# Norm's factor squared and applied after the down projections, seven products in another order, one plain block of features for two

## The chip, the cores and the metric

One core of a Trainium2 chip runs the whole program. The metric is the device time in microseconds (us) of one execution; the time before is the median of three runs.

## The reference, cut to what matters

A trunk of two layers runs on 768 tokens (512 and 256). Each layer is an attention block and then this block, in float32:

```python
    h = rmsnorm(x, ln_mlp[layer])          # x * rsqrt(mean(x*x)) * gain, over 1024 features
    x = x + jnp.square(jax.nn.relu(h @ w_up[layer])) @ w_down[layer]
return rmsnorm(x, ln_f)
```

`w_up` is 1024 x 4096, `w_down` 4096 x 1024. A token's factor r of the norm is positive, so square(relu(r*v)) = r*r*square(relu(v)).

## The kernel before, in words

Features lie on the 128 partitions, tokens in the free dimension: `x[k]` is 128 features by 768 tokens, k = 0 to 7. The tokens are two halves A and B of 384. Every float32 product is made of three matmuls on halves (hi x hi, hi x lo, lo x hi); `wsplit` (L76) makes weight halves `whi` on ACT (L80) and `wlo` on DVE (L81), `halve` (L114) makes those of activations (ACT L116, DVE L117).

**Up stage** (L820 to L955). 16 blocks `mp` of 256 features. A block of two by two (features, tokens) over two halves of the 1024 inputs is 8 plain products of 12 matmuls, or 7 by Strassen and Winograd's scheme (`product`, L855, matmuls at L861). The first two blocks are plain (L902), because the scheme's operands `comb[4..7]` are made meanwhile by `second` (L804, subtractions at L797, halves at L116 and L117); the other 14 are made from 7 products (L928 on). POOL makes the weight sums of a block (L846), DVE adds the products up in the tile `z` (adds at L869, L952; one ACT copy at L934), and `finish` (L875) follows: DVE's max with 0 and times R, the norm's factor of each token (L880), ACT's square (L882), a store to T in HBM from ACT's queue (L883), DVE's three sums `ta`, `tb` (L889 to L891) and two stores from POOL's queue (L893). R needs the sum of squares of all x: `nm.add` (squares on ACT at L147, adds on DVE at L152) stands ahead of the blocks, `rstd` (L161, L166, L167) and `bcast` (L185) between the halves of the plain blocks, R's copy at L177.

**Down stage** (L959 to L1052). Seven products in ORDER 1, 2, 7, 4, 5, 6, 3, each of NG = 4 steps of 48 matmuls (L1027) into four PSUM banks r. `operand` (L920) loads T and halves it (tile `th`, three buffers), `halves` (L993) halves weights (four `whi`, two steps' worth), `sums` (L987) makes POOL add into the kept weights in place (L991), so that a sum waits until DVE has read the weights for the product before. After a product's last step the four banks are folded into x (L1031 to L1048): 48 DVE instructions of 128x384 and 4 ACT copies in a layer.

**Ends.** Layer 0 goes on with splits of x (L119, L120) and the next norm's squares; `sq2` takes their tiles in turn from two tags, one of them "R". Layer 1 ends with `final`, half by half: the first half beside the steps of the last product, the second after it.

The instructions of each engine run in the order that the framework has chosen at compile time, by its own estimate of when each is ready and by the program's order; the trace shows it (DVE's rows of several blocks interleave).

Of the kernel before, what the change touches and what calls it, by code (L numbers as in the profile page):

```python
# [37 lines left out]
def kernel(ctx: ExitStack, tc: tile.TileContext, a: dict, y: bass.AP):  # L38
# [735 lines left out]
    def mlp(layer, src, o, x, es):  # L774
# [6 lines left out]
        sq = lambda: xo_tile("sq")  # L781
        two = [0]

        def sq2():
            two[0] ^= 1
            return xo_tile("sq") if two[0] else cpool.tile([P, NT], F32, tag="R", name="sq", bufs=1)

        nm = Norm(sq2)
# [82 lines left out]
        R, wait, done = [], [], list(range(FF // 256))  # L871

        T = [dram.tile([P, 7, ND, HT], F32, name=f"T{layer}_{i}") for i in range(NG)]

        def finish(z):  # L875
# [23 lines left out]
        ws = [weights(True) for _ in range(2)]  # L899
        for k in MO:  # L900
            nm.add(x[k])
        for w in ws:  # L902
# [10 lines left out]
            if len(wait) == 1:  # L913
                w2 = weights()
                second()
        R.append(nm.spread(rt))
# [11 lines left out]
        for mp in range(2, FF // 256):  # L928
            w = weights() if mp > 2 else w2
# [6 lines left out]
            if mp == FF // 256 - 1:  # L936
# [3 lines left out]
                ths = [operand(1, 0)]  # L940
            add(z12, one(6), z11)
            add(z11, p2, z11)
            if mp == 2:
# [5 lines left out]
            if mp == 2:  # L949
# [3 lines left out]
            add(z12, p5, z12)  # L953
            finish(z)
        g2s.close()  # L955
# [16 lines left out]
        def fetch(n, i):  # L972

            for rp in PR:
                off = (((layer * NG + i) * 4 + (11, 22, 21, 12).index(BLOCK[n])) * 2 + rp) * P * 1024
                if n in (1, 4) and (n, i) != (1, 0):
                    t = ch.tile([P, 1024], F32, tag="ch", name="ch", bufs=8)
                else:
                    third[0] += n != 1
                    if n == 1 or third[0] % 3 == 0:  # L980
# [18 lines left out]
        def fold(out, x_, op=ALU.add):  # L999
            add(out, out, x_, op)  # L1000

# [6 lines left out]
        for s, (n, i) in enumerate(steps):  # L1008
# [20 lines left out]
            if i == NG - 1:  # L1029
                for r, ps in enumerate(banks):  # L1030
                    x12, x11, x22, x21 = (xb(r, m_, sl) for m_ in PR for sl in (A, B))  # L1031
# [4 lines left out]
                    if n == 4:  # L1036
                        fold(x21, ps)
                    if n in (7, 5):
                        fold(x22, ps, ALU.subtract)
                    if n == 7:  # L1040
                        fold(x21, ps, ALU.subtract)
                    if n in (5, 3):
                        fold(x12, ps)
                    if n == 6:
                        fold(u[:, r], ps)
                        fold(x21, u[:, r], ALU.subtract)
                        fold(x22, u[:, r], ALU.subtract)
                        fold(x12, u[:, r])  # L1048
            if layer == 1 and n == 3 and i < NG - 1:
                last[0](i)  # L1050
            elif layer == 1 and n == 6 and i == NG - 1:
                last = [final(x, lambda: acs.tile([P, HT], F32, tag="sq", name="sq", bufs=4), s_) for s_ in (HT, 0)]  # L1052
# [8 lines left out]
        es = open_hl()  # L1061
        nxt, nn = [None] * KD, Norm(sq2)
# [8 lines left out]
    def final(x, sq, s):  # L1071
# [186 lines left out]
```

## Time and profile before

| | us |
|---|---|
| median of 3 runs (1742.3 to 1744.41) | 1743.85 |
| the profiled execution | 1743.15 |
| its span in the trace | 1741.4 |
| up stage, layer 0 (first L861 to first L1027) | 361.7 to 610.0 |
| down stage, layer 0 | 610.0 to 847.4 |
| up stage, layer 1 | 1238.5 to about 1488 |
| down stage, layer 1, and end | to 1741.4 |

PE is the matmul engine, PEld its weight loads, which run beside matmuls; DVE, ACT, POOL and SP are the other engines; a q behind a name is its queue of DMA issues. In a row of the timeline the bracket gives the idle time of the engine just before the row, and what ended it. "x4" is four instructions in one row.

### The profile page before, as it was taken

The numbers are of one execution on the slowest core, as the hardware profiler recorded it, in microseconds if no ns is written. First come the engines' busy times: TensorE is split into PE (matmuls) and PEld (weight loads), VectorE is DVE, ScalarE is ACT, GpSimd is POOL, SyncE is SP. The second block draws the span as 40 slices with busy tenths as digits, with TensorE's granted clock in tenths as the row PEclk, the third lists the DMA queues.
The fourth block names the chain that finished last, engine by engine and source line by source line (L and its number), as shares of the span: only waits on it lengthen the run. The fifth ranks groups of instructions, "written<-read, shape, count | busy, mean of one in ns | idle before, by whom it ended". The sixth has DMA issues, their size and how long they took to land.

```text
span 1741.4 us, 28288 instructions
## 1 busy us (share of the span) xinstructions
PE 1710.9 (98%) x10988; PEld 1622.0 (93%) x10988; DVE 1396.1 (80%) x2202; ACT 823.5 (47%) x1513; POOL 571.3 (33%) x435
## 2 busy tenths in 40 slices
PE   8999999999999999999999999999999999999997
PEld 8888888899999999999999999988999999999997
DVE  8888647499888888899566776775898898787994
ACT  7765434354333354444435555554543333544442
POOL 2200000034566414574021222210235655054751
PEclk9999999999999999999999999999999999999998
DMA  4111222414444687663310111112134445977621
GB/s 170 37 46 49 69 78 91 136 38 156 158 158 157 199 343 300 244 209 133 115 49 32 50 39 33 55 59 97 49 117 160 159 168 177 345 294 266 207 91 73
DMA packets 74597, 235.42 MB, mean 135 GB/s; under 512 B 7904, under 2 KB 25056, under 8 KB 74464
## 3 DMA queue, kind: packets, MB, share of 16 engines
q1 hardware_dynamic: 52480, 186.93, 31.4%
q0 software_dynamic: 7168, 25.17, 3.9%
q10 hardware_dynamic: 14816, 21.52, 3.4%
q8 instruction: 86, 1.41, 0.3%
q14 instruction: 47, 0.39, 0.1%
HBM read 182.47 MB, written 50.33 MB: 134 GB/s over the span
## 4 chain that ended last, share of the span: by engine, by line
PE 69%; DVE 19%; issue 6%; ACT 4%; POOL 1%; DMA 1%; POOLq 0%; DVEq 0%; ACTq 0%; SPq 0%
PE dn L1027 26%; PE dqk L196 8%; PE opa L208 5%; DVE z L880 4%; PE dvp L196 4%; DVE z L869 3%; DVE wlo L81 3%; PE npa L208 3%; PE opb L208 3%; DVE t L869 3%; DVE t L797 2%; ACT z L882 2%; PE ds L274 2%; PE dpv L721 2%; PE qp L196 2%
## 5 line engine op out<-in xcount | busy, mean ns | idle before, releaser
L861 PE MATMUL up<-c,whi 128*128 128x384 f32 x1824 | 467.3, 337 | 1.3 <-ACT z L911 1.3
L1027 PE MATMUL dn<-th,whi 128*128 128x384 f32 x1792 | 460.8, 338 | 0.0
L861 PEld LDWEIGHTS up<-c,whi 128*128 128x128 f32 x1824 | 330.3, 188 | 1.6 <-ACT z L911 1.5
L1027 PEld LDWEIGHTS dn<-th,whi 128*128 128x128 f32 x1792 | 325.7, 188 | 0.7 <-DVE th L117 0.5
L861 PE MATMUL up<-c,wlo 128*128 128x384 f32 x912 | 309.8, 340 | 4.9 <-DVE wlo L81 4.7
L1027 PE MATMUL dn<-th,wlo 128*128 128x384 f32 x896 | 302.9, 338 | 0.5 <-DVE wlo L81 0.5
L846 POOL TENSOR_TENSOR s<-wraw 128x512 f32<-128x512 f32 x56 | 104.1, 1877 | 420.3 <-DMA wraw<-in_w_up_dram 369.6
L991 POOL TENSOR_TENSOR ch<-ch,wd 128x1024 f32<-128x1024 f32 x60 | 189.1, 3161 | 117.0 <-DVE wlo L81 94.5
L81 DVE TENSOR_TENSOR wlo<-ch,whi 128x1024 fp32r<-128x1024 f32 x88 | 167.2, 1915 | 27.7 <-ACT whi L80 27.5
L861 PEld LDWEIGHTS up<-c,wlo 128*128 128x128 f32 x912 | 171.3, 188 | 12.4 <-DVE wlo L81 12.1
L80 ACT ACTIVATE whi<-ch 128x1024 fp32r<-128x1024 f32 x88 | 93.2, 1064 | 176.2 <-PE dn L1027 138.9
L1027 PEld LDWEIGHTS dn<-th,wlo 128*128 128x128 f32 x896 | 168.3, 188 | 1.1 <-DVE wlo L81 1.1
L117 DVE TENSOR_TENSOR th<-tr,th 128x1536 fp32r<-128x1536 f32 x56 | 142.3, 2544 | 12.0 <-ACT th L116 11.5
L81 DVE TENSOR_TENSOR wlo<-wraw,whi 128x1024 fp32r<-128x1024 f32 (+3 forms) x132 | 139.2, 1055 | 14.3 <-ACT whi L80 14.1
L80 ACT ACTIVATE whi<-wraw 128x1024 fp32r<-128x1024 f32 (+3 forms) x128 | 116.8, 914 | 55.3 <-PE opb L208 24.6
L882 ACT ACTIVATE z<-z 128x1536 f32<-128x1536 f32 x32 | 47.7, 1490 | 165.8 <-DVE z L880 165.8
L196 PE MATMUL dqk<-whi,xh 128*128 128x256 f32 x384 | 114.7, 299 | 0.0
L196 PE MATMUL dqk<-whi,xl 128*128 128x256 f32 x384 | 107.5, 280 | 0.0
L196 PE MATMUL dqk<-wlo,xh 128*128 128x256 f32 x384 | 107.2, 279 | 0.0
L706 ACT ACTIVATE de<-ds,m 128x512 f32<-128x512 f32 (+1 forms) x96 | 58.4, 613 | 81.7 <-DVE m L704 81.7
L116 ACT ACTIVATE th<-tr 128x1536 fp32r<-128x1536 f32 x56 | 82.7, 1477 | 23.2 <-DMA tr<-T 14.1
L869 DVE TENSOR_TENSOR z<-up,z 128x384 f32<-128x384 f32 x168 | 89.7, 548 | 0.1
(220 smaller groups left out, 3736.4 us busy)
## 6 DMA issues: line engine op xcount, KB each, us to landing
wd<-in_w_down_dram SPq DMA_DIRECT2D x84, 512.0 KB, 5.0
tr<-T SPq DMA_DIRECT2D x56, 768.0 KB, 5.6
wraw<-in_w_up_dram SPq DMA_DIRECT2D x64, 512.0 KB, 3.6
T<-t POOLq DMA_DIRECT2D x64, 384.0 KB, 3.0
T<-z ACTq DMA_DIRECT2D x32, 576.0 KB, 3.0
ch<-in_w_down_dram SPq DMA_DIRECT2D x28, 512.0 KB, 7.4
wraw<-in_w_in_o_dram SPq DMA_DIRECT2D x24, 512.0 KB, 3.6
wraw<-in_w_in_e_dram SPq DMA_DIRECT2D x16, 512.0 KB, 3.6
```

What stands on the lines that cost most here:

```text
L80: nc.scalar.activation(hi, raw, AF.Copy)
L81: nc.vector.tensor_tensor(out=lo, in0=raw, in1=hi.bitcast(F32), op=ALU.subtract)
L116: nc.scalar.activation(hi, src, AF.Copy)
L117: nc.vector.tensor_tensor(out=lo, in0=src, in1=hi.bitcast(F32), op=ALU.subtract)
L196: nc.tensor.matmul(ps[:, :256], st[:, tk], col(k, part, 0, 256), start=(k == 0 and i == 0), stop=(k == KD - 1 and i == 2))
L208: nc.tensor.matmul(ps[:, : e - s], w, mv[:, s:e], start=(k == 0 and i == 0), stop=(k == nk - 1 and i == 2))
L846: nc.gpsimd.tensor_tensor(out=d_, in0=x_, in1=y_, op=ALU.add)
L861: nc.tensor.matmul(ps, part[a_][:, base + k * P : base + (k + 1) * P], t[:, b_], start=start and k + i == 0, stop=stop and k == 3 and i == 2)
L869: nc.vector.tensor_tensor(out=out, in0=x_, in1=y_, op=op)
L882: nc.scalar.activation(z, z, AF.Square)
L991: nc.gpsimd.tensor_tensor(out=t, in0=t, in1=new.pop((i, rp)), op=ALU.add)
L1027: nc.tensor.matmul(ps, w[a_][:, c : c + P], th[:, b_, q], start=i + q + a_ + b_ == 0, stop=i == NG - 1 and q == ND - 1 and a_ == 1)
```

## The change

R is no longer applied to the up stage's `z`: `z` gets ACT's Relu and Square in place, and R squared (`R2`) multiplies the down stage's sums. One plain block is left of two, and 15 blocks are made from 7 products. `nm.add` goes, one a block, into blocks 4 to 11, `rstd` behind block 12, `bcast` and R2's two ACT squares behind the last block. The down products come in the order 4, 5, 6, 3, 1, 7, 2; they are gathered in `e`, `f`, `h` and go into x only after the multiplication by R2. Layer 0's `sq2` now shares the tag "R" with R2. In layer 1 half A is finished first.

```diff
-        nm = Norm(sq2)
+        nm = Norm(lambda: cpool.tile([P, NT], F32, tag="R", name="sq", bufs=1))
...
+        def square(z, relu=True):
+            if relu:
+                nc.scalar.activation(z, z, AF.Relu)
+            nc.scalar.activation(z, z, AF.Square)
...
-            nc.vector.scalar_tensor_tensor(out=z, in0=z, scalar=0.0, in1=R[0][:, None, :].broadcast_to([P, 2, NT]),
-                                           op0=ALU.max, op1=ALU.mult)
-            nc.scalar.activation(z, z, AF.Square)
...
-        ws = [weights(True) for _ in range(2)]
-        for k in MO:
-            nm.add(x[k])
+        ws = [weights(True) for _ in range(1)]
...
-                if last == 0 and wait:
-                    rt = nm.rstd()
...
-                nc.scalar.activation(z[:, i, sl], pss[n], AF.Copy)
+                nc.scalar.activation(z[:, i, sl], pss[n], AF.Relu)
+            square(z, False)
...
-        R.append(nm.spread(rt))
...
-                ths = [operand(1, 0)]
+                ths = [operand(4, 0)]
...
+            square(z)
             finish(z)
+            if 4 <= mp < 4 + KD:
+                nm.add(x[MO[mp - 4]])
+            elif mp == 4 + KD:
+                rt = nm.rstd()
+
+        R2 = cpool.tile([P, NT], F32, tag="R", name="R2", bufs=1)
+        for c in (0, 4):
+            pb = nm.bcast(rt, c)
+            nc.scalar.activation(R2[:, c * P : c * P + pb.shape[1]], pb, AF.Square)
...
-        u = acs.tile([P, 4, HT], F32, name=f"u_{layer}")
+        e, f, h = (acs.tile([P, 4, HT], F32, name=f"{n}_{layer}") for n in "efh")
-        ORDER = (1, 2, 7, 4, 5, 6, 3)
+        ORDER = (4, 5, 6, 3, 1, 7, 2)
...
+        def scaled(out, x_, sl):
+            rr = R2[:, sl] if len(x_.shape) == 2 else R2[:, None, sl].broadcast_to([P, 4, HT])
+            nc.vector.tensor_tensor(out=out, in0=x_, in1=rr, op=ALU.mult)
...
+                    if n == 4:
+                        nc.scalar.activation(f[:, r], ps, AF.Copy)
+                    if n == 5:
+                        nc.scalar.activation(h[:, r], ps, AF.Copy)
+                    if n == 3:
+                        add(e[:, r], ps, h[:, r])
+                    if n in (6, 1, 7):
+                        fold(f[:, r], ps, ALU.subtract)
+                        fold(h[:, r], ps)
                     if n == 1:
-                        nc.scalar.activation(u[:, r], ps, AF.Copy)
+                        fold(e[:, r], ps)
                     if n in (1, 2):
-                        fold(x11, ps)
...
+                        t = acs.tile([P, HT], F32, tag="t", name="t", bufs=4)
+                        scaled(t, ps, B)
+                        fold(xb(r, 0, B), t)
+                if n == 1:
+                    scaled(e, e, A)
+                    for r in range(4):
+                        fold(xb(r, 0, A), e[:, r])
+                if n == 7:
+                    scaled(h, h, A)
+                    for r in range(4):
+                        fold(xb(r, 1, A), h[:, r], ALU.subtract)
+                    scaled(f, f, B)
+                    for r in range(4):
+                        fold(xb(r, 1, B), f[:, r])
```

## Rows read from the trace of the kernel before

**Rows 1.** The page's busy time of each engine: us, share of the span, instructions.
```profile
span 1741.4 us, 28288 instructions
PE 1710.9 (98%) x10988; PEld 1622.0 (93%) x10988; DVE 1396.1 (80%) x2202; ACT 823.5 (47%) x1513; POOL 571.3 (33%) x435
```

**Rows 2.** Busy time by stretch: first the up and the down stage of layer 0, then three blocks of the up stage. Columns: stretch, its us, then busy us (instructions) of PE, PEld, DVE, ACT, POOL, granted clock, DMA share, GB/s.
```profile
405.00:610.00 205.00, 202.44 (x1144) 198.52 (x1143) 183.86 (x208) 78.83 (x83) 113.53 (x78) 1.00 0.51 174
610.00:847.00 237.00, 236.76 (x1344) 236.11 (x1344) 210.13 (x151) 109.83 (x102) 102.56 (x34) 1.00 0.64 233
...
510.00:555.00 45.00, 44.11 (x248) 42.70 (x248) 40.12 (x45) 16.74 (x18) 26.86 (x19) 1.00 0.45 157
```

**Rows 3.** What the weight loads of the up stage's matmuls (L861, both layers) sat idle for: releaser, us in total, times.
```profile
  DVE wlo L81: 12.1, 23
  ACT z L911: 1.5, 1
```

**Rows 4.** Weight loads in order of time, at the broadcast of the norm's factor, layer 0 and layer 1.
```profile
397.66 1.41 PEld L185 LDWEIGHTS pb<-ident,rt 128*128 128x128 f32 x12 [0.92 <-POOL rt L167]
...
1274.35 1.42 PEld L185 LDWEIGHTS pb<-ident,rt 128*128 128x128 f32 x12 [1.03 <-POOL rt L167]
```

**Rows 5.** DVE in order of time over one block of the up stage.
```profile
480.93 2.85 DVE L880 SCALAR_TENSOR_TENSOR z<-z,R 128x1536 f32<-128x1536 f32 x1
485.33 1.80 DVE L869 TENSOR_TENSOR t<-z 128x768 f32<-128x768 f32 x1 [1.55 <-ACT z L882]
...
488.24 0.55 DVE L869 TENSOR_TENSOR z<-up,z 128x384 f32<-128x384 f32 x1
488.71 1.22 DVE L81 TENSOR_TENSOR wlo<-wraw,whi 128x1024 fp32r<-128x1024 f32 x1
...
495.93 2.84 DVE L880 SCALAR_TENSOR_TENSOR z<-z,R 128x1536 f32<-128x1536 f32 x1
```

**Rows 6.** L880's and L882's instructions: duration in ns, least, median, most.
```profile
L880 DVE SCALAR_TENSOR_TENSOR z<-z,R x32: 1746/2846/2853, 404.8 to 1490.2; 128x1536 f32<-128x1536 f32 x32
L882 ACT ACTIVATE z<-z x32: 1476/1491/1496, 406.6 to 1492.0; 128x1536 f32<-128x1536 f32 x32
```

**Rows 7.** DVE in order of time from the plain blocks on, layer 0; the second part is a row of layer 1.
```profile
365.85 2.35 DVE L81 TENSOR_TENSOR wlo<-wraw,whi 128x1024 fp32r<-128x1024 f32 x2
368.13 3.01 DVE L152 TENSOR_TENSOR acc<-acc,sq 128x768 f32<-128x768 f32 x3
...
373.30 4.01 DVE L152 TENSOR_TENSOR acc<-acc,sq 128x768 f32<-128x768 f32 x2
377.24 1.65 DVE L797 SCALAR_TENSOR_TENSOR t<-x,gains,t 128x384 f32<-128x384 f32 x1
378.82 0.95 DVE L152 TENSOR_TENSOR acc<-acc,sq 128x768 f32<-128x768 f32 x1
379.69 0.61 DVE L797 SCALAR_TENSOR_TENSOR t<-x,gains,t 128x384 f32<-128x384 f32 x1
...
400.45 1.96 DVE L117 TENSOR_TENSOR c<-t,c 128x384 fp32r<-128x384 f32 x4
...
1254.59 2.04 DVE L152 TENSOR_TENSOR acc<-acc,sq 128x768 f32<-128x768 f32 x1
```

**Rows 8.** SP's queue: two loads of up weights (issued at 338.27 and at 345.35) ahead of the plain blocks; and POOL's first weight sums.
```profile
338.27 7.41 SPq L74 DMA_DIRECT2D wraw<-in_w_up_dram  x2
...
370.83 3.69 POOL L846 TENSOR_TENSOR s<-wraw 128x512 f32<-128x512 f32 x2 [283.97 <-DMA wraw<-in_w_up_dram]
```

**Rows 9.** Down stage, DVE and POOL in order of time: halves of two weights and of an operand beside POOL, an operand's without POOL, four folds beside POOL.
```profile
753.06 4.56 DVE L81 TENSOR_TENSOR wlo<-ch,whi 128x1024 fp32r<-128x1024 f32 x2
756.57 7.20 POOL L991 TENSOR_TENSOR ch<-ch,wd 128x1024 f32<-128x1024 f32 x2 [1.17 <-DVE wlo L81]
757.55 3.96 DVE L117 TENSOR_TENSOR th<-tr,th 128x1536 fp32r<-128x1536 f32 x1
...
689.40 1.76 DVE L117 TENSOR_TENSOR th<-tr,th 128x1536 fp32r<-128x1536 f32 x1 [0.15 <-ACT th L116]
...
712.69 1.94 DVE L869 TENSOR_TENSOR x<-x,dn 128x384 f32<-128x384 f32 x4
712.90 2.41 POOL L991 TENSOR_TENSOR ch<-ch,wd 128x1024 f32<-128x1024 f32 x1 [4.28 <-DVE wlo L81]
```

**Rows 10.** Start of the down stage in order of time: the last store of T, the load that waited for it, and its halves.
```profile
620.86 0.72 POOL L893 DMA_DIRECT2D T<-t  x1 [1.47 <-DVE t L869]
628.38 0.33 SPq L923 DMA_DIRECT2D tr<-T  x1
632.64 1.49 ACT L116 ACTIVATE th<-tr 128x1536 fp32r<-128x1536 f32 x1 [3.82 <-DMA tr<-T]
634.16 1.76 DVE L117 TENSOR_TENSOR th<-tr,th 128x1536 fp32r<-128x1536 f32 x1 [4.08 <-ACT th L116]
```

**Rows 11.** End of layer 0's down stage: the last add of the next norm's squares, and PE's sums of them behind the first 96 matmuls of the next layer.
```profile
851.70 0.95 DVE L152 TENSOR_TENSOR acc<-acc,sq 128x768 f32<-128x768 f32 x1
...
858.62 1.39 PE L161 MATMUL ss<-ones,acc 128*128 128x2 f32 x12
```

**Rows 12.** End of the kernel: DVE's last fold, and the weight loads that waited for ACT's square of it.
```profile
1728.09 0.55 DVE L869 TENSOR_TENSOR x<-x,dn 128x384 f32<-128x384 f32 x1 [0.41 <-PE dn L1027]
...
1729.26 0.30 PEld L161 LDWEIGHTS ss<-ones,sq 128*128 128x128 f32 x2 [1.17 <-ACT sq L1087]
```

More of the change, by code (lines that the diff above doesn't have):

```diff
@@ L869, in add @@
             nc.vector.tensor_tensor(out=out, in0=x_, in1=y_, op=op)
-        R, wait, done = [], [], list(range(FF // 256))
+        wait, done = [], list(range(FF // 256))
         T = [dram.tile([P, 7, ND, HT], F32, name=f"T{layer}_{i}") for i in range(NG)]
+        def square(z, relu=True):
+            if relu:
+                nc.scalar.activation(z, z, AF.Relu)
+            nc.scalar.activation(z, z, AF.Square)
         def finish(z):
@@ L926, in operand @@
             return th
-        for mp in range(2, FF // 256):
-            w = weights() if mp > 2 else w2
+        for mp in range(first_mp, FF // 256):
+            w = weights() if mp > first_mp else w2
             one = lambda n: product(bank(n), w[n], n)
@@ L939, in mlp @@
                 pa_ = g1s.enter_context(tc.tile_pool(name=f"dna{layer}", bufs=4, reuse_waits="tile"))
-                ths = [operand(1, 0)]
+                ths = [operand(4, 0)]
             add(z12, one(6), z11)
             add(z11, p2, z11)
-            if mp == 2:
+            if wait:
                 finish(wait.pop(0))
@@ L948, in mlp @@
             add(z12, p3, z12)
-            if mp == 2:
+            if wait:
                 finish(wait.pop(0))
@@ L975, in fetch @@
                 off = (((layer * NG + i) * 4 + (11, 22, 21, 12).index(BLOCK[n])) * 2 + rp) * P * 1024
-                if n in (1, 4) and (n, i) != (1, 0):
+                if n in (1, 4) and (n, i) != (4, 0):
                     t = ch.tile([P, 1024], F32, tag="ch", name="ch", bufs=8)
                 else:
-                    third[0] += n != 1
-                    if n == 1 or third[0] % 3 == 0:
+                    third[0] += n != 4
+                    if n == 4 or third[0] % 3 == 0:
                         t = wpool.tile([P, 1024], F32, tag="wraw", name="wd", bufs=3)
@@ L1044, in mlp @@
[L1044 to L1049, printed above, removed]
-                last[0](i)
-            elif layer == 1 and n == 6 and i == NG - 1:
-                last = [final(x, lambda: acs.tile([P, HT], F32, tag="sq", name="sq", bufs=4), s_) for s_ in (HT, 0)]
+                        t = acs.tile([P, HT], F32, tag="t", name="t", bufs=4)
@@ L1053, in mlp, with sq @@
+            if layer == 1 and n == 2 and i < NG - 1:
+                last[0](i)
+            elif layer == 1 and n == 7 and i == NG - 1:
+                tiles = iter([(e, r) for r in range(4)] * 4)
+                def sq():
+                    e_, r = next(tiles)
+                    return e_[:, r]
+                last = [final(x, sq, s_, R2[:, A]) for s_ in (0, HT)]
         if layer == 1:
@@ L1061, in mlp, with sq2 @@
         es = open_hl()
+        two = [0]
+        def sq2():
+            two[0] ^= 1
+            return xo_tile("sq") if two[0] else cpool.tile([P, NT], F32, tag="R", name="sq", bufs=1)
         nxt, nn = [None] * KD, Norm(sq2)
@@ L1091, in part @@
                         nm.parts.append(t)
-                if not s:
+                if s:
                     for k in ms[:3]:
@@ L1105, in part @@
                     if k in early:
-                        nc.gpsimd.tensor_tensor(out=yt, in0=yt, in1=R[:, sl], op=ALU.mult)
+                        nc.gpsimd.tensor_tensor(out=yt, in0=yt, in1=Rs, op=ALU.mult)
                     else:
@@ L1111, in final @@
         return part
-    accs = [None, None]
+    accs = [None]
     hs_ = open_hl()
```

33 lines of the change are left out of this document (9 added, 24 removed).

## The prediction

> **What bounds the kernel now.** I read the page's busy shares first: PE 98%, its weight loads 93%, DVE 80% [rows 1]. So PE sets the end wherever it doesn't wait, and the question is where it waits. The view of stretches answers it: in the down stage the weight loads are busy 236.1 of 237 us, in the up stage 198.5 of 205 [rows 2]. The view of line L861 says for what: of both up stages' idle time 12.1 us go to DVE's `wlo` and 1.5 to an ACT evacuation [rows 3]; the timeline adds 0.92 and 1.03 us in which the broadcast waits for the norm's factor [rows 4]. Together 15.55 us, all in stages that the change rebuilds.
>
> Why PE waits for `wlo` shows in one block's timeline. DVE is busy 40.12/3 = 13.4 us a block [rows 2] and idle 1.55 us behind ACT's square [rows 5]: 14.9 us. PE needs 84 weight loads at 198.52/1143 = 0.174 us [rows 2], 14.6 us. L880 starts 15.0 us apart [rows 5], so the up stage goes at DVE's pace. L880 is the largest piece: 2.85 us in the median, 1.75 at least [rows 6]; it is slow where POOL's sums run. PE's clock is granted at 1.00 in all these stretches [rows 2]; nothing in the sum is a matter of clock.
>
> **The change part by part.** The sum is made against the profiled execution's 1743.15 us (span 1741.4 and 1.75 around it); the median is 0.7 us above that, and I add the 0.7 at the end.
>
> *Fewer matmuls.* A plain block has 96, the other kind 84; one block of each layer changes kind: 24 matmuls x 0.174 = 4.2 us, on the path because PE is.
>
> *Steady blocks of the up stage.* DVE loses L880 (2.85 us a block), ACT gains a Relu. No Relu of 128x1536 is in the trace; the same engine's Square of that shape takes 1.49 us [rows 6], which I take for both ends, as only the function differs. DVE's sums now wait for two passes, 3.0 us and not 1.55. DVE's block becomes 13.4 - 2.85 + 3.0 = 13.5 us if it idles through both, 10.5 if other work fills them: under PE's 14.6 either way, so the 12.1 us go. ACT has 126 us idle of 205 [rows 2] as cover for 16 x 1.49 = 24 us; without it every Relu would push back the next block's `whi`. The Trainium skill (ScalarE: Activation LUTs, section "Rules for kernel authors") says to run relu and max on VectorE and not on ScalarE, which speaks against the move. The rows disagree for this type and shape: 1.49 us on ACT, 1.75 to 2.85 on DVE; left on DVE the pass would keep the block at 14.9 us, and the sum would lose the 12.1.
>
> *Norm moved into the blocks.* Its 12 and 12 small matmuls are only moved; the waits for the factor (1.95 us) and the evacuation's 1.5 go, since the factor is ready long before it is used. But 8 blocks a layer get an add on DVE of 0.95 us alone and 2.04 beside POOL [rows 7]: 13.5 becomes 14.5 to 15.6 against 14.6, so 0 to 1.0 us in 16 blocks, 0 to 16 in all. I take 2.5, near the low end, because the add can go into the 3.0 us in which DVE waits.
>
> *One plain block as cover.* `second` must have made the operands of product 6 when PE has done 96 matmuls, three products and most of the fourth: 361.7 + 141 x 0.174 = 386.2 in layer 0. DVE worked without a break from 365.85 to 402.4 [rows 7]. Of that go seven norm adds (3.01 + 4.01 + 0.95 + 0.95 = 8.9 us) and the second plain block's halves (2.35): end at 391.1, product 6's last operand three halves (1.5 us) before: 389.7, so 3.5 us late at worst. Without POOL beside it the 16 subtractions take 0.61 and not up to 1.65 us [rows 7]: 368.2 + 16 x 0.61 + 16 x 0.49 + 0.6 - 1.5 = 384.9, not late at all. POOL's sums for this block waited for a load until 370.83, but two loads that now hold its weights were issued at 338 and 345 [rows 8], so they run earlier and only the following block's sums are beside it. I take 1.2 us a layer, 2.4 (0 to 7).
>
> *Down stage.* The folds grow from 48 to 60 DVE instructions of 128x384, three of 128x1536 come in, and ACT's copies go from 4 to 8: 12 x 0.48 [rows 9] + 3 x 1.75 to 2.85 [rows 6] = 11 to 14 us of DVE a layer. DVE has 27 us idle of 237 [rows 2], which covers them in sum; where it does not, in place, is the last product but one. Behind product 1 stand 20 + 4 small ones and one large, 24 x 0.48 + 1.75 = 13.3 us, of which 6.3 fit beside its last three banks (12 matmuls each). What is left, 7.0, with two weight halves (1.22 each [rows 5]) and an operand (1.76 [rows 9]) makes 11.2 us; PE wants the second of these halves a step and a half after the product's end, 72 x 0.174 = 12.5 us. It fits by 1.3 us if POOL is quiet. POOL's sums follow DVE's reading of the weights before [rows 9], so product 7's run during product 1 and are over. I take 0.5 us for both layers (0 to 27, see the second rival).
>
> *Edges.* The load of the last quarter of T waits for POOL's last store, and its halves are done at 635.9 [rows 10], as step 3 of the first product begins (610.0 + 144 x 0.174 and its waits, 636): no slack. Relu takes L880's place in that chain, but POOL's sums now start in the first product, and an operand's half can take 3.96 for 1.76 [rows 9]: 0 to 4.4, I take 0.5. At the hand-over to layer 1 the squares that use the tag "R" wait for R2's last reader, at 848; some six adds of 0.95 and waits between them end at 857 to 860, and PE's sum of them stands at 858.6 [rows 11], where it was 6 us ahead: 0 to 3, I take 0.5. At the very end the last bank gets a multiplication ahead of its fold, 0.5 us on the chain that ends the kernel [rows 12].
>
> Sum: -4.2 - 15.55 + 2.5 + 2.4 + 0.5 + 0.5 + 0.5 + 0.5 = -12.85; 1743.15 - 12.85 = 1730.3, with the 0.7 **1731**.
>
> **The rivals.** *All cover holds.* The norm's adds, `second` and the burst cost nothing: -4.2 - 15.55 + 0.5 = -19.2, 1724.6. For it: DVE's 10.5 us a block; against: DVE has never had a quiet stretch at either place.
>
> *The up stage stays at DVE's pace.* The order chosen at compile time leaves the 3.0 us empty and puts the norm's adds on top, at half their price (8 us), and `second` comes 3.5 us late in each layer: -4.2 - 15.55 + 8 + 7 + 2 = -2.75, 1741. For it: the old order also left 1.55 us empty though DVE was the bound [rows 5].
>
> *Slower: the burst behind product 1 meets POOL.* If product 7's sums are still running then, eight folds between SBUF tiles go from 0.48 to 1.65, the large one from 1.75 to 2.85, the two halves from 1.22 to 2.28, the operand from 1.76 to 3.96 [rows 6, 7, 9]: 9.4 + 1.1 + 2.1 + 2.2 = 14.8 more, 26.0 against 12.5, 13.5 us late in each layer. Of the other terms -13.35 are left, so it decides from 6.7 us a layer, half of that price; the whole price gives 1743.85 - 13.35 + 27 = 1757, three quarters 1751. Against it: in the window of rows 9 folds from PSUM kept 0.48 beside POOL, and product 7's sums have all of product 1's 33 us to run. The Trainium skill (SBUF - State Buffer, section "Who interferes with whom") calls the ports that VectorE shares with GpSimd an exclusive lock. The trace agrees as far as it shows it: both engines are slow at once in rows 9, and the folds that read PSUM are not.
>
> **How the numbers follow.** Forecast 1731 (1727 to 1738): 0.62, as each of its small costs lies near an end that a row supports. All cover: 0.16. DVE's pace: 0.14. Slower: 0.08. The range leaves out the slower rival and a little below the best case: 1723 to 1743. A measurement here can tell about 0.2% (3.5 us) from no change, so faster means under 1740.4: the first two and a quarter of the third, 0.82; same: the rest of the third, 0.10; slower 0.08.
>
> **What would show it.** Right: L861 with 1356 matmuls a layer, its idle time for `wlo` down from 12.1 to some 2 to 3 us, blocks of 14.6 to 14.8 us, no row of PE waiting for `rt` in the up stage; a wait of 0 to 3 us for the operands of product 6; down stages still 237 us. Wrong: weight loads idle for `wlo` in the down stage behind product 1, a DVE block still at 15 us with idle time behind ACT's square, or over 5 us of PE's time lost ahead of the first block of 7 products.

## The result

The changed kernel takes 1749.44 us (median of 5 runs, 1748.66 to 1751.57), the kernel before beside it 1744.41 us (5 runs): a ratio of 1.0033, 95% interval 1.0019 to 1.0048. It is slower by 0.33%, where 1731 and "faster" were forecast; the range ended at 1743. All the ratios below are against runs of the kernel before on the same chip. The profiled execution of the changed kernel took 1750.86 us around a span of 1749.1, that is 7.7 us more span than before.

The page after, against [rows 1]: DVE lost 40 us, ACT gained 50, and PE has 24 matmuls less.

```profile
span 1749.1 us, 28353 instructions
PE 1708.8 (98%) x10964; PEld 1623.4 (93%) x10964; DVE 1356.3 (78%) x2214; ACT 874.0 (50%) x1553; POOL 568.7 (33%) x443
```

The same stretches as in [rows 2] (up stage, down stage, three blocks; same columns):

```profile
405.00:608.00 203.00, 203.00 (x1170) 202.69 (x1169) 156.24 (x200) 99.89 (x99) 107.25 (x81) 1.00 0.52 176
609.00:849.00 240.00, 235.68 (x1337) 234.71 (x1337) 211.81 (x153) 111.88 (x105) 109.14 (x34) 1.00 0.64 224
...
510.00:555.00 45.00, 45.00 (x259) 45.00 (x258) 33.47 (x45) 21.89 (x22) 24.36 (x20) 1.00 0.51 171
```

The weight loads, busy 42.7 of 45 us of three blocks before and 198.5 of 205 in the stage, are now without a gap in the steady up stage. The down stage, where 0.9 us of 237 were idle, has 5.3 of 240. The groups of weight loads, with the mean in ns and the idle time ahead of them, answer to [rows 3]:

```profile
L854 PEld LDWEIGHTS up<-c,whi 128*128 128x128 f32 x1808 | 328.1, 188 | 7.4 <-ACT c L116 5.0 <-DVE c L117 1.6 <-ACT whi L80 0.5
L1034 PEld LDWEIGHTS dn<-th,whi 128*128 128x128 f32 x1792 | 326.6, 188 | 4.6 <-DVE th L117 4.2 <-ACT th L116 0.3
L854 PEld LDWEIGHTS up<-c,wlo 128*128 128x128 f32 x904 | 170.2, 188 | 1.2 <-DVE wlo L81 1.2
L1034 PEld LDWEIGHTS dn<-th,wlo 128*128 128x128 f32 x896 | 168.7, 188 | 7.5 <-DVE wlo L81 7.5
```

The 12.1 us for `wlo` are down to 1.2; 7.4 us ahead of `whi`, most of it for `c`, the halves of the operands that `second` makes (the combinations), and 12.1 in the down stages (1.8 before) have come in their place. Cutting both spans at the first and last weight load of the two stages' lines (L861 and L1027 before, L854 and L1034 after) shows where the 7.7 us arise; the last column is the best version found below:

| stretch, us | before | after | difference | best version |
|---|---|---|---|---|
| start to up stage, layer 0 | 361.66 | 363.81 | +2.15 | 361.20 |
| up stage, layer 0 | 248.32 | 244.75 | -3.57 | 241.90 |
| down stage, layer 0 | 237.08 | 241.28 | +4.20 | 236.32 |
| attention of layer 1 | 391.17 | 392.25 | +1.08 | 391.51 |
| up stage, layer 1 | 249.53 | 243.94 | -5.59 | 241.90 |
| down stage, layer 1 | 239.77 | 247.13 | +7.36 | 238.99 |
| from the last load to the end | 13.83 | 15.94 | +2.11 | 15.65 |

The up stages gave 9.2 us, the down stages took 11.6, the edges 5.3. The weight loads that waited, in order of time (start, duration, in brackets the idle time and its releaser), name the places:

```profile
390.58 0.19 PEld L854 LDWEIGHTS up<-c,whi 128*128 128x128 f32 x1 [2.51 <-ACT c L116]
391.55 0.29 PEld L854 LDWEIGHTS up<-c,whi 128*128 128x128 f32 x1 [0.78 <-DVE c L117]
...
661.02 0.19 PEld L1034 LDWEIGHTS dn<-th,wlo 128*128 128x128 f32 x1 [1.49 <-DVE wlo L81]
671.58 0.19 PEld L1034 LDWEIGHTS dn<-th,wlo 128*128 128x128 f32 x1 [2.17 <-DVE wlo L81]
792.49 0.19 PEld L1034 LDWEIGHTS dn<-th,wlo 128*128 128x128 f32 x1 [1.63 <-DVE wlo L81]
...
1507.01 0.19 PEld L1034 LDWEIGHTS dn<-th,whi 128*128 128x128 f32 x1 [3.62 <-DVE th L117]
...
1672.99 0.19 PEld L1034 LDWEIGHTS dn<-th,wlo 128*128 128x128 f32 x1 [1.63 <-DVE wlo L81]
1734.78 0.30 PEld L161 LDWEIGHTS ss<-ones,acc 128*128 128x128 f32 x2 [1.44 <-DVE acc L1114]
```

**The start of the down stage.** POOL and DVE in order of time, layer 0:

```profile
617.04 3.25 POOL L993 TENSOR_TENSOR ch<-ch,wd 128x1024 f32<-128x1024 f32 x1 [0.25 <-DVE wlo L81]
...
630.90 18.39 POOL L993 TENSOR_TENSOR ch<-ch,wd 128x1024 f32<-128x1024 f32 x5
649.26 6.75 POOL L993 TENSOR_TENSOR wd<-wd 128x1024 f32<-128x1024 f32 x2
655.97 7.25 POOL L993 TENSOR_TENSOR ch<-ch,wd 128x1024 f32<-128x1024 f32 x2
```

```profile
646.96 6.77 DVE L81 TENSOR_TENSOR wlo<-ch,whi 128x1024 fp32r<-128x1024 f32 x2
653.66 3.97 DVE L117 TENSOR_TENSOR th<-tr,th 128x1536 fp32r<-128x1536 f32 x1
657.55 6.76 DVE L81 TENSOR_TENSOR wlo<-ch,whi 128x1024 fp32r<-128x1024 f32 x2
664.23 3.97 DVE L117 TENSOR_TENSOR th<-tr,th 128x1536 fp32r<-128x1536 f32 x1
```

A step of 48 weight loads takes PE 8.45 us. DVE needs 6.76 + 3.97 = 10.7 us for a step while POOL's sums run beside it without a break, so it falls behind from step to step until PE waits at 661. Products 5, 6 and 3 all need sums, and they now come second to fourth. Before, product 2, which needs none, came second: POOL's first sum of the stage began at 646.44, and DVE had a step at the same price of 10.7 us without a wait of PE:

```profile
646.44 3.12 POOL L991 TENSOR_TENSOR wd<-wd 128x1024 f32<-128x1024 f32 x1 [24.85 <-ACT u L1033]
...
661.02 6.77 DVE L81 TENSOR_TENSOR wlo<-wd,whi 128x1024 fp32r<-128x1024 f32 x2
667.72 3.96 DVE L117 TENSOR_TENSOR th<-tr,th 128x1536 fp32r<-128x1536 f32 x1
```

**Behind product 1**, DVE's queue in layer 0. The group of additions and multiplications that begins at 775 is through at 789.6, then come the operand's half and the splits, of which PE wants the first at 790.9:

```profile
785.54 1.75 DVE L1007 TENSOR_TENSOR e<-e,R 128x1536 f32<-128x1536 f32 x1
787.21 0.55 DVE L862 TENSOR_TENSOR x<-x,t 128x384 f32<-128x384 f32 x1
787.68 1.95 DVE L862 TENSOR_TENSOR x<-x,e 128x384 f32<-128x384 f32 x4
789.55 1.75 DVE L117 TENSOR_TENSOR th<-tr,th 128x1536 fp32r<-128x1536 f32 x1
791.22 2.35 DVE L81 TENSOR_TENSOR wlo<-ch,whi 128x1024 fp32r<-128x1024 f32 x2
```

Every duration is the undisturbed one and POOL's last sum before this ended at 771.8, so this is length of queue alone.

**Before the up stage.** Half as many up weights are loaded for plain blocks, so POOL's first sums start at 347 and no longer at 370.83 [rows 8]. They now run beside the last operand's half, which takes 1.94 us where it took 0.96 before, and PE waits 1.10 us for it (0.91 in layer 1):

```profile
348.40 1.94 DVE L117 TENSOR_TENSOR ol<-no,oh 128x768 fp32r<-128x768 f32 x1 [0.91 <-ACT oh L116]
```

In the kernels below that have two plain blocks again the sums start later (in the best version at 370.38) and this wait is gone.

**The clock.** Over 30 to 38 us, far ahead of the changed code, the granted clock was 1.00 in the profile before and 0.79 after (first fence before, second after). In both the weight loads had sat idle for 2.71 us just ahead of it. The same weight load that stood at 45.29 us before stands at 46.56, so 1.3 us of the +2.15 in the first line of the table are not the change's.

```profile
30.00:38.00 8.00, 6.25 (x53) 6.28 (x54) 6.89 (x41) 6.75 (x23) 4.60 (x11) 1.00 0.15 53
```

```profile
30.00:38.00 8.00, 6.50 (x42) 6.53 (x43) 5.96 (x34) 5.22 (x17) 4.33 (x10) 0.79 0.09 34
391.00:400.00 9.00, 8.47 (x42) 8.45 (x42) 8.32 (x19) 6.07 (x11) 0.62 (x1) 0.81 0.03 13
1507.00:1517.00 10.00, 9.99 (x48) 9.93 (x48) 10.00 (x3) 3.15 (x4) 9.79 (x4) 0.83 0.52 185
```

The other two are behind the waits at 391 and 1507: ten loads stand 0.32 us apart there, not 0.176, 1.4 us each time. Half the clock is the lower of the two levels (1.2 GHz).

### The profile page after: what moved, and what is told of

Its sections match the earlier page's. It is cut to its first block, busy times and chain, and to the rows that moved or that the text cites. A ratio compares the mean times of both kernels' runs of the same rounds, so it can differ in the third digit from the quotient of the medians.

```text
span 1749.1 us, 28353 instructions
## 1 busy us (share of the span) xinstructions
PE 1708.8 (98%) x10964; PEld 1623.4 (93%) x10964; DVE 1356.3 (78%) x2214; ACT 874.0 (50%) x1553; POOL 568.7 (33%) x443
## 3 DMA queue, kind: packets, MB, share of 16 engines
q8 instruction: 86, 1.41, 0.3%
## 5 line engine op out<-in xcount | busy, mean ns | idle before, releaser
L854 PE MATMUL up<-c,whi 128*128 128x384 f32 x1808 | 463.8, 338 | 5.4 <-ACT c L116 4.3
L1034 PE MATMUL dn<-th,whi 128*128 128x384 f32 x1792 | 461.6, 339 | 3.7 <-DVE th L117 3.7
L854 PEld LDWEIGHTS up<-c,whi 128*128 128x128 f32 x1808 | 328.1, 188 | 7.4 <-ACT c L116 5.0
L1034 PEld LDWEIGHTS dn<-th,whi 128*128 128x128 f32 x1792 | 326.6, 188 | 4.6 <-DVE th L117 4.2
L1034 PE MATMUL dn<-th,wlo 128*128 128x384 f32 x896 | 302.9, 339 | 5.9 <-DVE wlo L81 5.9
L854 PE MATMUL up<-c,wlo 128*128 128x384 f32 x904 | 304.1, 338 | 0.5 <-DVE wlo L81 0.5
L839 POOL TENSOR_TENSOR s<-wraw 128x512 f32<-128x512 f32 x60 | 92.8, 1553 | 412.5 <-PE npv L601 258.9
L993 POOL TENSOR_TENSOR ch<-ch,wd 128x1024 f32<-128x1024 f32 x52 | 174.7, 3375 | 86.3 <-DVE wlo L81 76.0
L81 DVE TENSOR_TENSOR wlo<-ch,whi 128x1024 fp32r<-128x1024 f32 x80 | 157.8, 1998 | 27.0 <-ACT whi L80 26.8
L1034 PEld LDWEIGHTS dn<-th,wlo 128*128 128x128 f32 x896 | 168.7, 188 | 7.5 <-DVE wlo L81 7.5
L854 PEld LDWEIGHTS up<-c,wlo 128*128 128x128 f32 x904 | 170.2, 188 | 1.2 <-DVE wlo L81 1.2
L81 DVE TENSOR_TENSOR wlo<-wraw,whi 128x1024 fp32r<-128x1024 f32 (+3 forms) x132 | 145.6, 1103 | 17.4 <-ACT whi L80 16.7
L80 ACT ACTIVATE whi<-ch 128x1024 fp32r<-128x1024 f32 x80 | 84.6, 1062 | 132.7 <-PE dn L1034 94.2
L80 ACT ACTIVATE whi<-s 128x1024 fp32r<-128x1024 f32 x60 | 63.8, 1064 | 118.6 <-PE up L854 106.8
L81 DVE TENSOR_TENSOR wlo<-s,whi 128x1024 fp32r<-128x1024 f32 x60 | 83.4, 1390 | 35.3 <-ACT whi L80 35.2
```

Source lines behind the costliest of these rows:

```text
L80: nc.scalar.activation(hi, raw, AF.Copy)
L81: nc.vector.tensor_tensor(out=lo, in0=raw, in1=hi.bitcast(F32), op=ALU.subtract)
L839: nc.gpsimd.tensor_tensor(out=d_, in0=x_, in1=y_, op=ALU.add)
L854: nc.tensor.matmul(ps, part[a_][:, base + k * P : base + (k + 1) * P], t[:, b_], start=start and k + i == 0, stop=stop and k == 3 and i == 2)
L993: nc.gpsimd.tensor_tensor(out=t, in0=t, in1=new.pop((i, rp)), op=ALU.add)
L1034: nc.tensor.matmul(ps, w[a_][:, c : c + P], th[:, b_, q], start=i + q + a_ + b_ == 0, stop=i == NG - 1 and q == ND - 1 and a_ == 1)
```

## The experiments

A ratio is the time over that of the kernel before, with its 95% interval. Waits are the idle times of the weight loads, as in the brackets above. The expectations count them from the start of the load ahead, 0.18 to 0.19 us more each time: their 2.69 + 0.97 us are the 2.51 and 0.78 above.

**Start of the down stage: the sums, the order, and the group.** Two kernels, one that leaves the second product's sums out and one with the old order:

```
             if n in (7, 5, 6, 3):
                 t = kept[i, rp]
+                if n == 5:
+                    new.pop((i, rp))
+                    continue
```

> Leaves out part of the computation: product 5's eight sums of weights on POOL in each layer (its matmuls take the block of product 4 as it is); the loads stay. Theory (DVE and POOL hold each other up in the first steps): the waits for wlo and th at 659 and 669 us (1.68 and 2.35 us) go, and 0.5 to 1.6 us in layer 1, whose longest wait (3.81 us, and 1.45 us at half clock behind it) stays, as that one is for T's piece, which landed 13.7 us after its issue behind 3.1 MB of weights. Time near 1749.4 - 5 = 1744.5. Rival (the transfers alone): both layers' waits stay within 1 us, time 1748.5 or more. Rival (POOL alone, the transfer's wait too): all 11 us of it go, time near 1740.

Ratio 1.0010 (1.0001 to 1.0018). Layer 0's two waits are gone (down stage 237.46 us), layer 1's came down to one of 1.60 us (242.14), and the two behind product 1 stayed (1.68 and 1.63). The theory held and was too small: in layer 1 2.02 of the longest wait's 3.62 us went too. The operand's load landed 13.7 us after its issue in both kernels; what the sums added is its half's duration (first row: the changed kernel, second: this one), and the 1.60 us that are left stay with the late load:

```profile
1503.18 3.77 DVE L117 TENSOR_TENSOR th<-tr,th 128x1536 fp32r<-128x1536 f32 x1 [3.21 <-ACT th L116]
```

```profile
1501.23 1.76 DVE L117 TENSOR_TENSOR th<-tr,th 128x1536 fp32r<-128x1536 f32 x1 [5.20 <-ACT th L116]
```

How late the load is differs from kernel to kernel: with the same down stage behind another start (the last kernel of the next part) it landed after 9.7 us at most, and the waits were 2.05 and 1.80.

```
-        ORDER = (4, 5, 6, 3, 1, 7, 2)
+        ORDER = (1, 2, 7, 4, 5, 6, 3)
...
+                if n == 6:
+                    for w_, m_, s_, op in ((e, 0, A, ...), (h, 1, ...), (f, 1, B, ...)):
+                        scaled(w_, w_, s_)
+                        for r in range(4):
+                            fold(xb(r, m_, s_), w_[:, r], op)
```

> Undoes the order of the down projection's products: 1, 2, 7, 4, 5, 6, 3 as in the kernel before, with the squared factor still applied to the products' sums (the accumulators filled accordingly: e from products 1, 5, 6, h from 7, 1, 5, 6, f from 4 and h, 6; products 1, 2, 3 scaled one by one); the up stage as in the changed kernel. Theory (order): what the down stages lost, 4.20 and 7.36 us, comes from product 5's sums on POOL in the first steps; with the old order they return to 237 to 238 and 240 us, but for the larger group of additions and multiplications, which now stands behind product 6 (12 additions of 384 columns, three multiplications of 1536, 12 additions: some 17 us of DVE, where the group behind product 1 took 13.7 and cost 1.82 us): +2 to 4 us a layer. Time near 1749.4 - 11.6 + 6 = 1744. Rival (T's last quarter and the loads come late whatever the order): the first steps still wait 4 and 6 us and the time is 1749 to 1753.

(In this run h is scaled for, and added to, the other half of the tokens; the shapes are the same.) Ratio 1.0062 (1.0050 to 1.0074): slower than the changed kernel. The forecast fell by its second half only. At the start nothing waited in layer 0 and 0.57 us in layer 1; but the group behind product 6 cost 5.48 and 5.47 us and not 2 to 4 a layer, with half clock behind both:

```profile
827.00 0.29 PEld L1034 LDWEIGHTS dn<-th,wlo 128*128 128x128 f32 x1 [5.48 <-DVE wlo L81]
...
1706.17 0.29 PEld L1034 LDWEIGHTS dn<-th,wlo 128*128 128x128 f32 x1 [5.47 <-DVE wlo L81]
```

So the group had to be dealt out, one bank a step, once in the new order (over product 7's steps) and once in the old (over product 3's):

```
+            if n == 7:
+                r, ps = late.pop(0)
+                fold(f[:, r], ps, ALU.subtract)
+                fold(h[:, r], ps)
+                fold(e[:, r], ps)
...
```

> The changed kernel, but with the group of additions and multiplications behind product 1 (13.7 us of DVE, in front of the halves and weight splits of the next steps) dealt out over the four steps of product 7, one bank in each. Theory (queue order on DVE): the waits for wlo behind product 1 (1.82 us in each layer at 790 and 1671 us) go, and nothing else moves: down stages 239.5 and 245.3 us, 3.6 us less than the changed kernel, a ratio to the kernel before of 1.0012. Rival (DVE's load as a whole in these steps, with POOL's sums beside it): the same work late in smaller waits, 1.0033 as the changed kernel.

Ratio 1.0028 (1.0019 to 1.0037). The two waits of 1.63 us are gone, as the theory had it; the waits at the start of the stage stayed (1.84 and 2.17 in layer 0, 2.22 and 1.41 in layer 1). The time does not show the gain: the interval holds the rival's 1.0033 and not the theory's 1.0012. This profile has half clock in four places ahead of its end, the changed kernel's in three; how much of the missing time that explains is open.

> The old order of products (1, 2, 7, 4, 5, 6, 3) with the squared factor on the sums, and the large group behind product 6 dealt out: f's part at once (four additions, one multiplication, four additions), those of e and h over the four steps of product 3. Without the dealing out, the old order had no wait at the start of the down stages, but one of 5.49 and 5.5 us behind product 6 with stretches at half clock behind each. Theory (order and queue): both kinds of wait go, down stages 236.5 to 238 and 239.5 to 241 us, as in the kernel before; up stages as in the changed kernel. Ratio to the kernel before 0.997 to 0.999. Rival (the burst's work is too much for DVE wherever it stands): waits of 2 us or more stay in product 3's steps, ratio 1.002 or more.

Ratio 0.9985 (0.9976 to 0.9993): the theory, with down stages of 236.30 and 239.69 us, one wait of 0.76 us left in them. The four kernels with either order and the group whole or dealt out show it together: only with the old order and the group dealt out do the down stages come back, so the new order and the undivided group are what they lost.

**Start of the up stage.** PE waits for the second set of combinations there. First the two suspects by themselves:

```
-        ws = [weights(True) for _ in range(1)]
+        ws = [weights(True) for _ in range(2)]
```

> Undoes one part of the change: the first 512 features again as two plain blocks, all else as in the changed kernel. Theory (cover lost): with one plain block PE comes to the second set of combinations too early; in the changed kernel's profile it waits 2.69 + 0.97 us in layer 0, with the clock at half for 3.41 us right after (1.4 us), and 2.66 + 0.97 us in layer 1. Two plain blocks give 24 matmuls x 0.174 = 4.2 us back and take these 8.7 us away: both up stages near 242.5 + 2 us, the time near 1749.4 - 8.7 + 4.2 = 1745. Rival (the order of DVE's queue): the running sum's additions stand ahead of the combinations whatever covers them, the waits shrink by less than 2 us a layer, and the time is 1749 to 1753.

```
-            if 4 <= mp < 4 + KD:
+            if 6 <= mp < 6 + KD:
...
```

> Moves one thing: the norm's eight squares and seven additions start at block 6 and not at block 4, so that none stands ahead of the second set of combinations in DVE's queue (in the changed kernel three do, at 370 to 376 us, with 1.28 us of waits for ScalarE among them: 4.9 us). Theory (norm's additions): the combinations come some 4.9 us earlier, the waits of 3.66 and 3.63 us go and the half clock behind the first with them: both up stages 239.5 to 241 us where they were 244.75 and 243.94, the time near 1749.4 - 8.7 = 1741. Rival (DVE and POOL contend over the combinations: five of them took 1.17 us each, where one alone takes 0.55): over 2 us of each wait stay, and the time is 1747 or more.

Both theories fell. With two blocks the ratio was 1.0062 (1.0050 to 1.0074): no wait for combinations, but 3.01 + 0.96 us in layer 0 (3.41 + 0.96 in layer 1) for the next block's splits, which stood behind two of the norm's squares in ACT's queue (the second, held by DVE's addition, began at 405.03, the split at 405.78, and PE went on at 406.87). Starting the norm two blocks later gave 1.0042 (1.0030 to 1.0054) and the same waits, 2.50 + 0.79 us: the order fixed at compile time had put three of the seven additions where they were. Only tiles that come free late, on top of the start at block 6, moved them:

```
-        nm = Norm(lambda: cpool.tile([P, NT], F32, tag="R", ...))
+        nm = Norm(lambda: g1.tile([P, 2, HT], F32, tag="c0", ...))
```

> The changed kernel with the norm's seven additions truly behind the second set of combinations: their squares go to tiles that come free only after the plain block, and in the queue of DVE the first addition stands in block 7. (Starting them at block 6 alone had left three of seven where they were, and the wait too.) Theory (norm's additions ahead of the combinations): 4.9 us of DVE leave the stretch before the combinations, PE's waits at the start of the up stages (2.69 + 0.97 us and 2.66 + 0.97 us) go to under 0.5 us, and the half clock behind them with them: up stages 240 to 241 us, ratio to the kernel before 1.0033 - 8/1744 = 0.9987. Rival (one plain block is too short a cover for the combinations with POOL's sums beside them): at least 2 us of each wait stay, ratio 1.002 or more.

Ratio 1.0026 (1.0016 to 1.0035), the rival: 1.76 + 0.78 us stay in layer 0. DVE's rows, and two of ACT's, say why:

```profile
370.09 1.22 DVE L81 TENSOR_TENSOR wlo<-s,whi 128x1024 fp32r<-128x1024 f32 x1
373.98 0.69 DVE L81 TENSOR_TENSOR wlo<-wraw,whi 128x512 fp32r<-128x512 f32 x1 [2.67 <-ACT whi L80]
376.64 5.07 DVE L790 SCALAR_TENSOR_TENSOR t<-x,gains,t 128x384 f32<-128x384 f32 x5 [1.97 <-ACT t L803]
381.64 1.95 DVE L117 TENSOR_TENSOR c<-t,c 128x384 fp32r<-128x384 f32 x4
```

```profile
373.32 0.63 ACT L80 ACTIVATE whi<-wraw 128x512 fp32r<-128x512 f32 x1 [5.50 <-PE up L854]
375.61 0.49 ACT L902 ACTIVATE z<-up 128x384 f32<-128x384 f32 x1 [1.66 <-PE up L854]
```

Without the additions DVE sits idle for ACT, 4.6 us, and the combinations begin 11.9 us after the stage's start, as in the changed kernel (375.74). The additions had filled a hole. ACT was held by PE in turn: a split and the plain block's evacuation, which wait for PE's plain block, stand in its queue ahead of its first step for the combinations (376.00). Two more kernels on this one:

> Leaves out part of the computation: POOL's four sums of weights for the second seven-product block of each layer (that block's weights are taken from the blocks as loaded), on top of the norm's additions placed behind the combinations. With them PE waited 1.95 + 0.97 us for the combinations. Theory (DVE and POOL hold each other up: beside these sums five combinations took 1.17 us each, alone they take 0.55): the combinations come 3 us earlier, the waits fall under 0.5 us a layer, up stages 239.5 to 240.5 us, ratio 1.0026 - 0.0033 = 0.9993. Rival (DVE's own work is too long for one plain block): 2 us or more of the waits stay, ratio 1.002 or more.

Ratio 1.0012 (1.0004 to 1.0021). The five combinations took 2.73 us and not 5.07, and PE's wait for them fell to 0.22; but 0.96 + 0.90 us appeared at the splits of a later block, and the up stages stayed at 242.28 and 242.24 us. Neither theory has that: the wait moved.

> The changed kernel with the norm's additions behind the combinations, and the first 512 features again as two plain blocks. With the additions behind and one plain block PE still waited 1.95 + 0.97 us in layer 0 and 1.92 + 0.97 us in layer 1; with two plain blocks and the additions ahead it had waited for weight splits. Theory (cover): PE comes 16.7 us later to the combinations, none of these waits is left, and 24 matmuls x 0.174 = 4.2 us are paid for 5.8: up stages near 241.6 us (242.5 - 2.9 + 2.1), ratio to the kernel before 1.0026 - 0.0009 = 1.0017. Rival (DVE is behind for the whole start, the wait only moves to the next block's splits): over 2 us of waits stay in each layer's start, up stages 244 us or more, ratio 1.004 or more.

Ratio 0.9994 (0.9986 to 1.0003), up stages 241.90 and 241.89, no wait over 0.1 us left in them. Its time does not differ from the kernel before. So 12 matmuls more a layer cost less than what they cover. Its groups of weight loads:

```profile
L854 PEld LDWEIGHTS up<-c,whi 128*128 128x128 f32 x1824 | 330.4, 188 | 0.1
...
L854 PEld LDWEIGHTS up<-c,wlo 128*128 128x128 f32 x912 | 171.3, 188 | 0.0
```

**The parts together.**

> The two together: the old order of products with the group dealt out, and the norm's additions behind the combinations. If each theory holds: up stages 240 to 241 us, down stages 237 and 240 us, tail and the stretch before the up stages as in the changed kernel (+2 us and +1 us); 1744.4 - 16.5 - 1 + 4 = 1731, a ratio of 0.992 to 0.994. If only the order's theory holds 0.997, if neither 1.002.

Ratio 0.9956 (0.9941 to 0.9970); up stages 242.45 and 242.39, down stages 236.30 and 238.99. The order's part held, the norm's did not, as above. From here four kernels looked for the rest, the second on top of the first, the other two on this one:

```
-            if n == 3:
+            for _ in range((2, 1, 1, 0)[i] if n == 3 else 0):
```

> The version with the old order, the group dealt out and the norm's additions behind the combinations, but with the pieces of e and h dealt to product 3's steps as 2, 1, 1, 0 and not 1, 1, 1, 1, so that the last step carries only its own four multiplications and four additions. Theory: PE's last wait (3.29 us before the sums of squares, where the changed kernel had 1.62 and the kernel before 1.36) falls to 1.6, the time by 1.6 us, ratio 0.9956 - 0.001 = 0.9947. Rival (the wait is for the squares on ScalarE): no change in it, 0.9956. Nothing moves elsewhere.

0.9962 (0.9950 to 0.9974): nothing, the wait ahead of PE's sums of squares is 3.10 us as it was. It is not the dealt-out pieces that hold it.

> The same as the version with the pieces dealt 2, 1, 1, 0, and in the first seven-product block the four products that read the second set of combinations go through k together (the quarter of the features that is ready first for all four, then the next), not one product after the other: DVE makes the combinations quarter by quarter, and the first product otherwise needs all four quarters at once. Theory (the order in which PE asks for them): the waits of 1.94 + 0.97 and 1.91 + 0.97 us at the start of the up stages go, up stages 239.5 to 240.5 us, ratio 0.9947 - 0.0033 = 0.991. Rival (the last quarter, and the next block's splits behind it in DVE's queue, set the time whatever PE asks for first): the wait moves to the next block, up stages within 1 us of 242.4, ratio 0.994 to 0.995.

0.9952 (0.9940 to 0.9964): the rival. 0.75 + 0.79 us of waits for combinations are left in layer 0, and 0.46 for the next splits are new; up stages 241.97 and 242.33.

```
+        second((0, 1))
         for n_, w in enumerate(ws):
...
-                second()
+                second((2, 3))
```

> The version with the old order, the group dealt out, the norm's additions behind the combinations and one plain block, but with the combinations of the first two of the four quarters written ahead of the plain block, so that ScalarE's first steps for them stand ahead of the next block's weight split and of the plain block's evacuation in its queue. Theory (the wait is for ScalarE's queue): in the version so far DVE sat idle 2.67 us behind that weight split and 1.97 us behind ScalarE's first step, which itself came 1.66 us behind PE's first bank; without the additions there was nothing to fill this time with, so taking them away moved the combinations by nothing. Started 7 us earlier, in time that DVE has idle, they are done before PE asks: the waits of 1.94 + 0.97 and 1.91 + 0.97 us go, up stages 239.5 to 240.3 us, ratio 0.9956 - 0.0033 = 0.992. Rival (POOL's sums beside the combinations are what makes them late): they run beside them as before, the waits stay over 1.5 us a layer, ratio 0.995 or more.

0.9967 (0.9957 to 0.9978): the rival again. The combinations began at 368.54 and the first five took 2.73 us, but POOL's sums came later too, at 381.57 for 371.69, and met the last two quarters:

```profile
384.36 3.22 DVE L117 TENSOR_TENSOR c<-t,c 128x384 fp32r<-128x384 f32 x2
387.50 1.65 DVE L790 SCALAR_TENSOR_TENSOR t<-x,gains,t 128x384 f32<-128x384 f32 x1
```

PE waited 0.68 + 0.66 + 0.83 us in layer 0 and 2.94 + 1.15 in layer 1. Three ways to reorder this start (additions, PE's order, earlier combinations) and one that took POOL's sums away each shortened the wait or moved it; only the second plain block, with the additions behind, removed it.

> The part of the change that moves the factor, alone: the squared factor on the products' sums, with the old order of products (the group dealt out), the norm's additions behind the combinations, and two plain blocks as in the kernel before. Theory (256 features plain cost more than they give): the waits of 1.94 + 0.97 and 1.91 + 0.97 us at the starts of the up stages go, POOL's sums no longer run beside the last operand's halves before the stage (about 1 us, layer 0; 1.1, layer 1), 4.2 us of matmuls come back: up stages 241.9 us, down stages 236.3 and 239 us; 3 to 4 us less than with one plain block, ratio to the kernel before 0.9935 to 0.995. Rival (with the old order the one plain block is worth its 4.2 us): ratio 0.996 or more.

Ratio 0.9933 (0.9920 to 0.9947), 1729.85 us: the best version, faster than both kernels. It keeps the part of the change that moves the factor, with the norm's additions spread over later blocks and the group dealt out, and neither the one plain block nor the new order. Its up, down and down stage (columns as in [rows 2]) have no gap in the weight loads:

```profile
405.00:603.00 198.00, 198.00 (x1144) 198.00 (x1143) 151.22 (x197) 99.72 (x101) 98.04 (x75) 1.00 0.51 173
604.00:839.00 235.00, 235.00 (x1337) 234.92 (x1336) 209.73 (x163) 109.46 (x101) 101.53 (x34) 1.00 0.62 224
1472.00:1711.00 239.00, 239.00 (x1372) 238.93 (x1372) 210.49 (x173) 107.79 (x106) 105.47 (x35) 1.00 0.59 213
```

## Why the prediction was wrong

**Fewer matmuls, steady blocks: right.** 4.2 us of matmuls went, and of the 15.55 us of waits 1.7 are left (1.2 `wlo`, 0.5 `whi`); no wait for the factor. Relu took 1.49 us on ACT, the value taken from Square, and three blocks fill 45.00 of 45 us with weight loads. The norm's additions cost the steady blocks nothing where 2.5 was taken. By itself this part is what the best version shows: 241.9 us a stage, with the 96 matmuls.

**One plain block as cover: mis-sized.** 2.4 us were taken, 3.29 and 3.25 measured, and 1.4 at half clock behind the first. The working's own worst case, 3.5 a layer, was the right end. It was left because POOL's sums would "run earlier and only the following block's sums are beside it". They did, at 347, and cost PE 1.10 and 0.91 us there, a place without a term; and the following block's sums alone sufficed to double the first five combinations. Of the seven additions that the sum took away three stayed ahead; and DVE did not work without a break once they were away too: the sum took what DVE was busy with for what it was held by, and ACT's queue held it for 4.6 us.

**Start of the down stage: the step that failed most.** 0.5 us (0 to 4.4) were taken for both layers, against 3.66 us of waits in layer 0, and in layer 1 5.2, with 1.4 more at half clock. The step saw that "POOL's sums now start in the first product", and priced one operand half beside them. It should have asked for a step's DVE work at the disturbed durations, 2 x 3.4 + 3.97 = 10.7 us, against PE's 8.45, and for how many steps that lasts. By [rows 9] alone (two splits in 4.56, an operand in 3.96) a step is 8.5 us, just PE's pace, because POOL pauses there between its sums; the full price stood in the trace before at 661, outside the rows that the working used. The order of the products says that none without sums now stands between the first and theirs. DVE's 27 idle us in the stage were an average over steps with and without POOL. In layer 1 the late load of the operand is 1.60 us of the 5.2, as the kernel without product 5's sums shows.

**The burst behind product 1: the right place, mis-sized.** 0.5 us were taken, 3.26 measured. Two things were off. The deadline: PE wanted the first of the two splits 9.9 us after the product's end (781.0 to 790.9), not 12.5, which is when it wants the second. And the work: by the working's numbers the first was done 11.2 - 1.2 = 10.0 us after that end; it took 11.4, as a second operand's half of 1.75 us stood inside the group. The slower rival's price, POOL beside the group, did not come about, as argued: POOL was quiet. In the old order the longer group cost 5.5 a layer.

**Hand-over: nothing**, where 0.5 was taken; the +1.08 in the table is layer 1's wait ahead of the up stage. **Tail:** 2.1 us for 0.5. The multiplication and one addition of squares that now stands ahead of the last fold make about 1 us of it, and the sums of squares ran at half clock after a wait of 1.44:

```profile
1733.70 0.56 DVE L1007 TENSOR_TENSOR t<-dn,R 128x384 f32<-128x384 f32 x1 [0.15 <-PE dn L1034]
1734.18 0.55 DVE L1114 TENSOR_TENSOR acc<-acc,e 128x384 f32<-128x384 f32 x1
1734.64 0.55 DVE L862 TENSOR_TENSOR x<-x,t 128x384 f32<-128x384 f32 x1
```

**The cases.** "Slower" had 0.08 for one mechanism at one place. What came was a sum of five places with 2 to 9 us each over both layers: three had a range in the working and were taken near its low end, the tail was priced at a quarter, and the wait ahead of the up stage had no term. That 1749 lies near the slower rival's 1751 is chance, as that rival's mechanism did not come. The time's distance to 1731 is 18 us; the best version, without the new order, the undivided group, the one plain block and the early additions, is 0.0100 below the changed kernel's ratio, 17 us. Open is what each of the waits' half-clock stretches costs in the median run, since a wait of the same length has it in one profile and not in another.

## What to carry to other kernels

Where two engines slow each other down (here VectorE and GpSimd), compare an engine's work for one step at the disturbed durations with the step, not its busy share with the stage; and when an order of steps changes, list for each new neighbour what it brings to the engines at that place. When work is taken out ahead of a late result, look at what that result itself waits for: it may have filled a hole. A group of small instructions that is dealt out over the next steps can cost nothing where it cost 5.5 us in one piece.

## What the runs showed of the hardware

The granted clock is not a function of the wait ahead of it. After waits of 2.51 and 0.78 us for `c` in layer 0 of the changed kernel it was granted at half (1.2 GHz), after 2.47 and 0.78 us in layer 1 it was not; after the 2.7 us near 31 us it was in 7 of the 16 profiles and not in the other 9. In the best version, where the stages have no such waits, it was 1.00 in all of them. The Trainium skill (TensorE: Matmul & The Clock Gate, section "What's actually happening") says of a kernel's first matmuls that it differs from run to run how many of them run at the lower clock; these traces show the like behind waits in the middle of a kernel.

DVE instructions with two inputs from SBUF slowed down beside POOL's sums, and the sums with them: 0.55 us became 1.17 in the combinations, 1.75 became 3.97 in the operand's half, 1.22 became 3.4 in a split, and POOL's own sum went from 2.41 to 3.6. The Trainium skill (SBUF — State Buffer, section "Who interferes with whom") says that such an instruction contends with a GpSimd one that reads SBUF; the trace agrees, and adds that both lose.
